# A bound by one broadcast minimum, and a subtraction moved into the bias of the exponentials, in the scan of a hybrid diffusion trunk

## The chip, the cores and the metric

The kernel runs on one core of a Trainium2 chip (trn2). The metric is the device time of one execution, in microseconds (us). Engines are named as in the profile: PE is TensorE, PEld its weight loads, DVE is VectorE, ACT is ScalarE, POOL is GpSimd, and SP issues the DMAs.

## The reference

Two layers over 512 latent and 256 context tokens with 1024 channels: layer 0 mixes tokens by a bidirectional Mamba-2 scan (SSD), layer 1 by neighbourhood attention, and each is followed by a squared-ReLU MLP. The part that matters here is one chunk of 128 tokens of the scan. Per direction there are 32 heads in 4 groups of 8; `dtc` is the step size after the softplus and `a` is negative, so `cum` falls along a chunk:

```python
cum = jnp.cumsum(dtc * a, axis=1)
seg = cum[:, :, None] - cum[:, None, :]
decay = jnp.exp(jnp.where(mask, seg, -jnp.inf))
cb = jnp.einsum('bign,bjgn->bijg', cc, bc)
scores = cb[..., None] * decay * dtc[:, None]
y = jnp.einsum('bijge,bjgep->bigep', scores, xc)
```

## The kernel before

Tokens lie in the free dimension and channels on partitions, in 6 chunks of 128 tokens. All large products are made of three float32r products of split operands: a unit of weights (1024 rows, 128 columns) comes by DMA as `raw`, ACT rounds it to `wh` (L112), and DVE subtracts to get `wl` (L113); PE then runs 48 matmuls on it (L137), 24 with 512 columns and 24 with 256. `wh` and `wl` have two buffers each, so the split for a unit waits until PE has left the unit two before it.

The SSD layer walks the units of the input projection, `w_in`. A unit ends in a convolution and Silu (`conv_unit`, L542 to L549) or in a Silu and a gate (`z_unit`, L681, then `gate`, L670 to L675). Between the matmuls of each unit, `unit` advances a generator, `scan`, by three steps. So the scan of one group of heads runs beside the projections of the next. A scan has 29 steps; the last 18 hold the work inside the chunks, three for each chunk.

Inside a chunk the weights are formed by `decays`, for four heads and both directions at once, so 12 times for each group and 48 times in all. The tile `E` is [128, 2, 4, 128]: partition j, direction, head, token i. Two DMAs (L609) fetch `cum` of the tokens i for four heads, from `crow` in DRAM, spread over all partitions. Eight DVE instructions (L613), one for each direction and head, subtract the column `colb` = cum_j - ln dt_j and take the minimum with the column `lnd` = ln dt_j; without that bound the masked half could overflow. One ACT instruction (L615) takes the exponential of all 1024 columns. Then `G`, the masked product of C and B, is multiplied in, for direction 0 by DVE (L616) and for direction 1 by POOL (L617), and POOL adds the two (L618). PE multiplies the sum by the inputs `xtok` (L639). `E` has three buffers, and a call of `decays` is made one ahead of its use.

Beside it a chunk has: the product of the carried states `sf` and `sb` with C (L651, fp32), its scaling by `eb` (L653, DVE), the sum `y` (L655 DVE, L657 POOL), the inputs weighted for the next state (`xw`, L582, POOL), their product (L584) and the state's step (L594, L595, DVE).

The order on each engine is fixed when the program is built, by a scheduler that works from the program's order and its own estimates; weight splits go ahead with high priority. The engine queues run in that order, so an instruction that waits holds all that stands behind it.

Of the kernel before, what the change touches and what calls it, by code (L numbers as in the profile page):

```python
# [7 lines left out]
F32 = mybir.dt.float32  # L8
# [5 lines left out]
P = 128  # L14
# [14 lines left out]
# column layout of the small-parameter array  # L29
# [7 lines left out]
# column layout of the constants  # L37
# [3 lines left out]
# order in which the column blocks of ssd_w_in (past dt) are walked  # L41
XBC_ORDER = []
for _g in range(GROUPS):
    XBC_ORDER += [16 + _g, 24 + _g, 20 + _g, 28 + _g]  # B fwd, B bwd, C fwd, C bwd
    XBC_ORDER += [4 * _g + _i for _i in range(4)]
# blocks whose residual sums go to GpSimd
# [5 lines left out]
def trunk(ctx: ExitStack, tc: tile.TileContext, a, out, dbg=None, stop=None):  # L52
# [14 lines left out]
    def psum(**tags):  # L67
        """Cuts PSUM anew: a pool per tag, of the given number of buffers."""
        if psums:
            psums["stack"].close()  # L70
        psums["stack"] = st = ctx.enter_context(ExitStack())
        for tag, bufs in tags.items():
            psums[tag] = st.enter_context(tc.tile_pool(name=f"ps_{tag}", bufs=bufs, space=bass.MemoryType.PSUM))
# [18 lines left out]
    # rows 0, 32 and 64 are ones: spreads row 32 j of a tile over all partitions  # L92
# [23 lines left out]
    class Units:  # L116
        """Walks the 128-column units of a weight array."""
# [24 lines left out]
    def ln_exp_tables(after):  # L142
        """Loads the table set with both Ln and Exp once the instruction `after` is issued."""
# [4 lines left out]
    # silu(c) and silu(c_ctx), side by side for each block of 128 channels  # L148
# [8 lines left out]
    def mod_unit(ps, q, raw):  # L157
        """Unit q of the weights of a chunk of 512 columns: half q // 2 of the columns, blocks 4 (q % 2) + j of the rows,
        whose products go to the partitions 32 j and 32 j + 1 (and others into those behind), so that the four run at once."""
# [6 lines left out]
    def mod_finish(l, ch, ps, cp, row_pool=None):  # L166
        """The four parts of the sums ps plus the bias, into columns."""
# [24 lines left out]
    def mod_pieces(chunks, pool_):  # L192
        """The same in four pieces a chunk, as a generator that yields after each."""
# [18 lines left out]
    def mod(l, i, s):  # L212
        """Column [128, 8] of modulation term i for stream s (0 latent, 1 context)."""
# [12 lines left out]
    def scaled(name, l, n, i, plus1):  # L226
        """g[n] * (m_i + 1) or g[n] * m_i, as [128, 8, 2]."""
# [6 lines left out]
    def rsqrt_into(r, t, ms):  # L234
        """r = ms^-1/2 where ms holds mean + eps already; t is scratch."""
# [6 lines left out]
    # Values per token are kept on [96, 256]: tokens 256 j .. on partitions 32 j .. 32 j + 31.  # L242
    xsq = const.tile([96, 256], F32, name="xsq")  # mean square of the residual stream
# [4 lines left out]
    def row_sums(ps, js, terms):  # L248
        """ps [96, 256], rows j = sums over the partitions and over the terms [128, 256] that terms(j) lists, for j in js."""
# [10 lines left out]
    def spread(js, src, into):  # L260
        """into[:, tokens j] = row j of src, on all partitions."""
# [5 lines left out]
    class Sums:  # L267
        """Sums over the blocks of a sub-layer's output y, per partition and token: y^2, x y' and y'^2, where
        y' = y times the column factors and x the residual stream. The last block's share stays apart."""
# [6 lines left out]
        def add(self, o, y, yp, x, G, s0, s1, final=False):  # L276
            """Block o: yp[:, o] = y * G, and the sums."""
# [13 lines left out]
        def factors(self, js, pre=None, final=False):  # L291
            """R and r for the token ranges js: x + y' R is the stream after the sub-layer, r the factor of its
            rmsnorm. Moves xsq on. pre: y still lacks the factor pre per token."""
# [9 lines left out]
            else:  # L303
                # rmsnorm(pre * v) = v * pre / sqrt(pre^2 mean(v^2) + eps)
# [23 lines left out]
    def add_block(k, y, x, R, sl):  # L328
        """x += y' R for block k and the tokens sl."""
# [4 lines left out]
    def modulate(k, b, x, r, A, sh, s, hh, hl):  # L334
        """hh + hl = x * r * A + sh for block k; b is scratch."""
# [4 lines left out]
    def join(y, x, sums, sl, A, s, hh, hl):  # L340
        """x += y' R, hh + hl = x A for the tokens sl. What the norm still wants, times r and plus the shift, comes behind
        the product with the weights."""
# [17 lines left out]
    def shift_cols(l, i, at, hh, hl):  # L360
        """The columns at and at + 1 of hh + hl: the shifts of both streams."""
# [14 lines left out]
    # ================= layer 0: mixer input =================  # L376
# [58 lines left out]
    # ================= layer 0: SSD =================  # L435
# [12 lines left out]
    # dt: softplus, decays  # L448
    colb = dk.tile([P, NCH, 64], F32, name="colb")
    lnd = dk.tile([P, NCH, 64], F32, name="lnd")  # L450
# [19 lines left out]
    # log1p(e) = 2 atanh(e / (2 + e))  # L470
# [17 lines left out]
    dve.scalar_tensor_tensor(dta, dtv, -1.0, arow.unsqueeze(1).broadcast_to([P, NCH, 64]), ALU.mult, ALU.mult)  # L488
    lndf = lnd.rearrange("p c q -> p (c q)")
    dve.tensor_scalar(lndf, dt, 1.0e-37, None, op0=ALU.max)  # L490
    act.activation(lndf, lndf, AF.Ln)
    # running sums inside each chunk: forward from its start, backward from its end
# [4 lines left out]
    cum = ssd.tile([P, NCH, 64], F32, tag="sf", name="cum", bufs=2)  # L497
# [9 lines left out]
    dve.tensor_tensor(colb, cum, lnd, ALU.subtract)  # L507
# [21 lines left out]
    def unit(acc, n):  # L529
        """One unit of w_in, with n steps of the scan on the way."""  # L530
# [6 lines left out]
    def conv_unit(xb, tag, bufs, n=3):  # L537
        """One 128-channel block of silu(conv(h @ w_in) + b)."""
# [746 lines left out]
```

## Time and profile before

| what | value |
|---|---|
| runs shown | 2261.58 us median of 3 (2261.01, 2261.58, 2269.79) |
| span of the profiled execution | 2267.4 us; its own time isn't listed apart from the three runs, whose range the span lies in |
| PE busy over the span | 94% |
| DVE, ACT, POOL busy | 59%, 41%, 24% |
| mean granted clock of PE | 0.967 |

The span counts from the first to the last instruction. Busy shares are averages over stages: the scan stage takes the time from about 100 to 700 us, then come the MLP of layer 0, the attention and the second MLP. The rows below name lines by their numbers in the kernel before; those of the changed kernel lie one or two lines further down.

### The profile page before, as it was taken

What the parts mean: (1) busy time and instruction counts of PE and PEld (TensorE: products, weight loads), DVE (VectorE), ACT (ScalarE), POOL (GpSimd) and SP (SyncE); (2) the same over time, 40 slices, a digit from 0 to 9 for tenths busy, and PEclk for the clock granted to TensorE, in tenths of its full rate; (3) what the DMA queues carried; (4) which work ended last, traced back from release to release, by engine and by line L of the source; (5) the groups of instructions that cost most, each with busy time, mean ns of one, the idle gap of its engine ahead of it and who ended that gap; (6) DMA issues with size and microseconds to landing.
All of it is one profiled execution on the core that took longest, in us unless ns stands there. A gap on an engine that the chain in (4) does not pass through costs nothing.

```text
span 2267.4 us, 32646 instructions
## 1 busy us (share of the span) xinstructions
PE 2135.5 (94%) x12848; PEld 1761.0 (78%) x12848; DVE 1337.9 (59%) x2311; ACT 931.3 (41%) x1405; POOL 552.5 (24%) x434
## 2 busy tenths in 40 slices
PE   6999999989979988999999999799999989999996
PEld 3787777867868766888888888578788768899896
DVE  5758878688584787314334244677666665344355
ACT  4544534544333653223123134355555543333244
POOL 0024645253462562000000003612212170000003
PEclk8999999999999998999999999799999899999998
DMA  7436757366565622333333111321110124222233
GB/s 262 137 131 187 211 167 215 112 176 189 182 184 188 213 75 75 112 112 113 116 114 110 61 65 58 112 69 35 54 52 33 38 75 140 93 93 92 95 103 112
DMA packets 136877, 269.73 MB, mean 119 GB/s; under 512 B 13074, under 2 KB 70804, under 8 KB 136724
## 3 DMA queue, kind: packets, MB, share of 16 engines
q1 hardware_dynamic: 136724, 267.65, 37.2%
q8 instruction: 101, 1.65, 0.3%
q14 instruction: 52, 0.43, 0.1%
HBM read 244.27 MB, written 23.33 MB: 118 GB/s over the span
## 4 chain that ended last, share of the span: by engine, by line
PE 77%; DVE 12%; POOL 3%; issue 3%; DMA 3%; ACT 2%; SPq 0%; DVEq 0%; ACTq 0%; POOLq 0%
PE acc L826 20%; PE acc L878 20%; PE acc L137 17%; PE a L965 5%; DVE E L613 4%; PE a L976 2%; DMA E<-crow 2%; PE sc L1023 2%; PE s L162 2%; PE pt L1037 1%; PE yp L1052 1%; PE sc L1022 1%; DVE wl L113 1%; PE s L584 1%; PE s L253 1%
## 5 line engine op out<-in xcount | busy, mean ns | idle before, releaser
L112 ACT ACTIVATE wh<-raw 128x1024 fp32r<-128x1024 f32 (+1 forms) x241 | 254.2, 1055 | 688.3 <-PE acc L878 311.2
L113 DVE TENSOR_TENSOR wl<-raw,wh 128x1024 fp32r<-128x1024 f32 (+1 forms) x241 | 316.7, 1314 | 242.7 <-ACT wh L112 239.6
L137 PE MATMUL acc<-hh,wh 128*128 128x512 f32 (+1 forms) x976 | 289.5, 373 | 0.0
L137 PE MATMUL acc<-hl,wh 128*128 128x512 f32 (+1 forms) x976 | 264.3, 346 | 0.0
L137 PE MATMUL acc<-hh,wl 128*128 128x512 f32 (+1 forms) x976 | 262.4, 344 | 0.0
L826 PE MATMUL acc<-hh,wh 128*128 128x258 f32 (+2 forms) x1024 | 243.2, 317 | 9.8 <-ACT hh L357 9.8
L878 PE MATMUL acc<-ah,wh 128*128 128x512 f32 (+1 forms) x832 | 248.2, 348 | 4.1 <-DVE ya L884 4.0
L878 PE MATMUL acc<-ah,wl 128*128 128x512 f32 (+1 forms) x832 | 245.3, 344 | 0.8 <-DVE wl L113 0.8
L878 PE MATMUL acc<-al,wh 128*128 128x512 f32 (+1 forms) x832 | 245.6, 345 | 0.0
L826 PE MATMUL acc<-hl,wh 128*128 128x258 f32 (+2 forms) x1024 | 241.8, 314 | 3.1 <-DVE hl L358 3.0
L826 PE MATMUL acc<-hh,wl 128*128 128x258 f32 (+2 forms) x1024 | 240.9, 313 | 0.0
L137 PEld LDWEIGHTS acc<-hh,wh 128*128 128x128 f32 (+1 forms) x976 | 156.6, 191 | 54.5 <-issue 36.5
L613 DVE TENSOR_SCALAR E<-E,colb,lnd 128x128 f32<-128x128 f32 x384 | 171.8, 506 | 35.1 <-DMA E<-crow 34.9
L826 PEld LDWEIGHTS acc<-hh,wh 128*128 128x128 f32 x1024 | 161.2, 192 | 33.9 <-issue 11.5
L289 POOL TENSOR_TENSOR syy<-syy,last 128x512 f32<-128x512 f32 (+2 forms) x24 | 38.1, 1588 | 582.2 <-ACT last L279 582.1
L826 PEld LDWEIGHTS acc<-hl,wh 128*128 128x128 f32 x1024 | 160.9, 191 | 17.4 <-DVE hl L358 5.0
L137 PEld LDWEIGHTS acc<-hh,wl 128*128 128x128 f32 (+1 forms) x976 | 153.9, 190 | 25.0 <-issue 1.4
L137 PEld LDWEIGHTS acc<-hl,wh 128*128 128x128 f32 (+1 forms) x976 | 154.5, 191 | 23.9 <-issue 0.8
L826 PEld LDWEIGHTS acc<-hh,wl 128*128 128x128 f32 x1024 | 161.9, 191 | 11.7 <-issue 0.7
L878 PEld LDWEIGHTS acc<-ah,wh 128*128 128x128 f32 x832 | 140.2, 190 | 32.8 <-issue 13.1
L884 DVE TENSOR_TENSOR ya<-ya,acc 128x768 f32<-128x768 f32 (+2 forms) x56 | 40.6, 725 | 198.0 <-PE acc L878 198.0
L878 PEld LDWEIGHTS acc<-ah,wl 128*128 128x128 f32 x832 | 140.2, 189 | 21.8 <-DVE wl L113 1.0
(317 smaller groups left out, 3837.2 us busy)
## 6 DMA issues: line engine op xcount, KB each, us to landing
raw<-in_w_dram SPq DMA_DIRECT2D x136, 512.0 KB, 3.4
mraw<-in_modw_dram SPq DMA_DIRECT2D x72, 512.0 KB, 3.3
raw<-in_win_dram SPq DMA_DIRECT2D x48, 512.0 KB, 3.9
E<-crow SPq DMA_DIRECT2D x96, 256.0 KB, 5.2
eb<-erow SPq DMA_DIRECT2D x96, 128.0 KB, 3.7
raw<-in_wout_dram SPq DMA_DIRECT2D x24, 512.0 KB, 3.4
raw<-in_modw_dram SPq DMA_DIRECT2D x8, 1024.0 KB, 17.6
raw<-in_wqk_dram SPq DMA_DIRECT2D x16, 512.0 KB, 3.3
```

The costliest lines, as they stand in the source:

```text
L112: act.activation(wh[:, :n], raw[:, :n], AF.Copy)
L113: dve.tensor_tensor(wl[:, :n], raw[:, :n], wh[:, :n].bitcast(F32), ALU.subtract)
L137: pe.matmul(acc[:m, s0:s1], lhsT=ww[:, i * m:(i + 1) * m], rhs=xx[:, k, s0:s1], start=first and i == 0 and j == 0, stop=last and i == len( ...
L162: mm = pe.matmul(ps[32 * j:32 * j + 32, hf * 256:hf * 256 + 256], lhsT=cact[:, 8 * kg + 2 * j:8 * kg + 2 * j + 32], rhs=raw[:, j * 256:j * ...
L289: pool.tensor_tensor(t[:, s0:s1], t[:, s0:s1], d, ALU.add)
L613: dve.tensor_scalar(E[:, d, e], E[:, d, e], colb[:, c, q:q + 1], lnd[:, c, q:q + 1], op0=ALU.subtract, op1=ALU.min)
L826: pe.matmul(acc[:, d0:d0 + s1 - s0], lhsT=ww[wi], rhs=xx[:, k, s0:s1], start=k == 0 and j == 0, stop=k == KB - 1 and j == 2)
L878: pe.matmul(acc[:, s0:s1], lhsT=ww[:, k * P:(k + 1) * P], rhs=xx[:, s0:s1], start=k == 0 and j == 0, stop=k == KB - 1 and j == 2)
L884: dve.tensor_tensor(y, y, acc[:, p0:p1], ALU.add)
L965: pe.matmul(acc[:, :s1 - s0], lhsT=ws[ww][:, k * P:(k + 1) * P], rhs=xx[:, k, s0:s1], start=k == 0 and j == 0, stop=k == KB - 1 and j == 2)
L976: pe.matmul(acc, lhsT=xx[:, k, i * P:(i + 1) * P], rhs=w[ww][:, sl], start=k == 0 and n == 0, stop=k == KB - 1 and n == 2)
L1023: pe.matmul(ps[:, o:o + 256], lhsT=Q[2][own, qs], rhs=K[par][own, ks], start=False, stop=True)
```

## The change

`decays` bounds the exponent before the subtraction instead of behind it: min(cum_i, cum_j) is taken for all 1024 columns in one DVE instruction, with `cum` of the partition's own token as an operand that is repeated along i (a stride of zero). The rest of the exponent, `ncol` = ln dt_j - cum_j, is a value per partition, direction and head, and goes into the exponential as its bias; one ACT instruction then covers only the 128 columns of one head and direction, so there are eight. The product with `G` is one DVE instruction over 1024 columns, and POOL keeps the sum alone. For the tiles, `cum` takes the place of `lnd` among those that are kept, and `ncol` that of `colb`.

```diff
-    colb = dk.tile([P, NCH, 64], F32, name="colb")
-    lnd = dk.tile([P, NCH, 64], F32, name="lnd")
+    ncol = dk.tile([P, NCH, 64], F32, name="ncol")
+    cum = dk.tile([P, NCH, 64], F32, name="cum")
...
+    lnd = ssd.tile([P, NCH, 64], F32, tag="sf", name="lnd", bufs=2)
...
-    cum = ssd.tile([P, NCH, 64], F32, tag="sf", name="cum", bufs=2)
...
-    dve.tensor_tensor(colb, cum, lnd, ALU.subtract)
+    dve.tensor_tensor(ncol, lnd, cum, ALU.subtract)
...
             E = ssd.tile([P, 2, 4, P], F32, tag="E", name="E", bufs=3)
             for d in range(2):
                 q0 = d * 32 + g * 8 + hf * 4
                 sp.dma_start(E[:, d], crow[c, q0:q0 + 4].partition_broadcast(P))
+            h0 = g * 8 + hf * 4
+            own = cum[:, c].rearrange("p (d q) -> p d q", d=2)[:, :, h0:h0 + 4].unsqueeze(3)
+            dve.tensor_tensor(E, E, own.broadcast_to([P, 2, 4, P]), ALU.min)
             for d in range(2):
                 for e in range(4):
-                    q = d * 32 + g * 8 + hf * 4 + e
-                    dve.tensor_scalar(E[:, d, e], E[:, d, e], colb[:, c, q:q + 1], lnd[:, c, q:q + 1],
-                                      op0=ALU.subtract, op1=ALU.min)
-            act.activation(E, E, AF.Exp)
-            dve.tensor_tensor(E[:, 0], E[:, 0], G[c][:, 0:1].broadcast_to([P, 4, P]), ALU.mult)
-            pool.tensor_tensor(E[:, 1], E[:, 1], G[c][:, 1:2].broadcast_to([P, 4, P]), ALU.mult)
+                    q = d * 32 + h0 + e
+                    act.activation(E[:, d, e], E[:, d, e], AF.Exp, bias=ncol[:, c, q:q + 1], scale=1.0)
+            dve.tensor_tensor(E, E, G[c].unsqueeze(2).broadcast_to([P, 2, 4, P]), ALU.mult)
             pool.tensor_tensor(E[:, 0], E[:, 0], E[:, 1], ALU.add)
```

The scheduler then sets other orders. In the scan of the second group, beside the second of its `z_unit` calls, DVE's queue (wl is the next weight split, zt the gate, y, eb and sf the chunk's output and state) stood before as:

```order
L113 TENSOR_TENSOR wl_3097<-raw_3094,wh_3096 128x1024
L613 TENSOR_SCALAR E_3042<-E_3042,colb_421,lnd_422 128x128 x4
L670 TENSOR_TENSOR zt_2940<-zt_2940,sq_2942 128x768
L655 TENSOR_TENSOR y_2999<-y_2999,s_2902 128x512
L613 TENSOR_SCALAR E_3042<-E_3042,colb_421,lnd_422 128x128 x3
L653 TENSOR_TENSOR eb_2897<-eb_2897,s_3001 128x512
L613 TENSOR_SCALAR E_3042<-E_3042,colb_421,lnd_422 128x128
L653 TENSOR_TENSOR eb_2897<-eb_2897,s_3007 128x512
L613 TENSOR_SCALAR E_3112<-E_3112,colb_421,lnd_422 128x128
L595 TENSOR_TENSOR sf_3021<-sf_3021,s_3019 128x512
L613 TENSOR_SCALAR E_3112<-E_3112,colb_421,lnd_422 128x128 x4
L616 TENSOR_TENSOR E_3042<-E_3042,G_2307 128x512
```

and now stands as:

```order
L113 TENSOR_TENSOR wl_3077<-raw_3074,wh_3076 128x1024
L613 TENSOR_TENSOR E_2956<-E_2956,cum_422 128x1024
L671 TENSOR_TENSOR zt_2922<-zt_2922,sq_2924 128x768
L656 TENSOR_TENSOR y_2980<-y_2980,s_2885 128x512
L654 TENSOR_TENSOR eb_2880<-eb_2880,s_2982 128x512
L613 TENSOR_TENSOR E_3023<-E_3023,cum_422 128x1024
L654 TENSOR_TENSOR eb_2880<-eb_2880,s_2988 128x512
L595 TENSOR_TENSOR sf_3002<-sf_3002,s_3000 128x512
L618 TENSOR_TENSOR E_2956<-E_2956,G_2295 128x1024
L613 TENSOR_TENSOR E_3092<-E_3092,cum_422 128x1024
L618 TENSOR_TENSOR E_3023<-E_3023,G_2295 128x1024
L113 TENSOR_TENSOR wl_3213<-raw_3210,wh_3212 128x1024
```

The pieces of the old minimum lay spread between the other instructions; the new ones are whole, and a third call's minimum has moved ahead of the next weight split. ACT's queue at the same place was:

```order
L112 ACTIVATE wh_3096<-raw_3094 128x1024
L681 ACT_TABLE_LOAD
L681 ACTIVATE zt_2940<-acc_2823 128x768
L674 ACTIVATE sq_2942<-zt_2940 128x768
L615 ACT_TABLE_LOAD
L615 ACTIVATE E_3042<-E_3042 128x1024
L615 ACTIVATE E_3112<-E_3112 128x1024
L112 ACTIVATE wh_3234<-raw_3232 128x1024
```

and is now:

```order
L112 ACTIVATE wh_3076<-raw_3074 128x1024
L682 ACT_TABLE_LOAD
L682 ACTIVATE zt_2922<-acc_2807 128x768
L617 ACT_TABLE_LOAD
L617 ACTIVATE E_2956<-E_2956,ncol_421 128x128
L675 ACTIVATE sq_2924<-zt_2922 128x768
L617 ACTIVATE E_2956<-E_2956,ncol_421 128x128 x7
L617 ACTIVATE E_3023<-E_3023,ncol_421 128x128 x8
L617 ACTIVATE E_3092<-E_3092,ncol_421 128x128 x6
L112 ACTIVATE wh_3212<-raw_3210 128x1024
```

Where two exponentials stood between two splits of weights, 22 stand now, of two whole calls and most of a third. Over the program ACT's queue holds 70 table loads, and held 58.

## Rows read from the trace of the kernel before

**Rows 1.** The page: busy time of each engine, its share of the span, instructions

```profile
PE 2135.5 (94%) x12848; PEld 1761.0 (78%) x12848; DVE 1337.9 (59%) x2311; ACT 931.3 (41%) x1405; POOL 552.5 (24%) x434
```

**Rows 2.** Busy time by engine in the four scan stretches together, all instructions

```profile
sum 311.40, PE 268.39 PEld 213.30 DVE 276.94 ACT 140.78 POOL 178.16; mean PE 67.10 PEld 53.33 DVE 69.23 ACT 35.19 POOL 44.54
```

**Rows 3.** The same stretches, instructions on tile E alone: length, busy (count), then PEclk, DMA

```profile
195.60:268.00 72.40, 6.35 (x72) 3.93 (x72) 35.60 (x79) 9.20 (x9) 29.85 (x18) 0.95 0.77 222
300.50:371.30 70.80, 5.87 (x72) 3.75 (x72) 39.14 (x72) 8.48 (x8) 23.30 (x15) 0.95 0.66 197
455.00:547.00 92.00, 8.16 (x88) 5.18 (x88) 49.70 (x90) 10.60 (x10) 30.35 (x18) 0.91 0.68 189
611.00:687.20 76.20, 7.20 (x82) 4.51 (x80) 38.14 (x72) 8.47 (x8) 26.75 (x16) 0.96 0.66 183
```

**Rows 4.** Chain of work inside the stretch 455 to 547 us, shares by line

```profile
by line: DVE E L613 26.9%; DMA E<-crow 14.6%; issue 10.4%; PE acc L137 6.1%; PE s L651 5.7%; POOL E L618 5.5%; DVE eb L653 4.8%; DMA eb<-erow 4.1%; PE s L639 3.9%; DVE wl L113 3.1%; DVE sf L595 2.6%; POOL ssqy L675 2.0%; DVE sf L594 2.0%; D
```

**Rows 5.** Waits of PE, 90 to 720 us: line, releaser, total, times, longest

```profile
PE s L639 <- POOL E L618: 33.0, 16, 5.3
```

**Rows 6.** Timeline of PE, 488 to 530 us: start, duration, line, [idle before, releaser]

```profile
508.12 1.12 PE L639 MATMUL s<-E,xtok 128*64 128x128 f32 x8 [5.32 <-POOL E L618]
...
517.72 0.52 PE L137 MATMUL acc<-hl,wh 128*128 128x512 f32 x2
...
522.30 0.51 PE L137 MATMUL acc<-hh,wl 128*128 128x512 f32 x2
...
524.06 0.66 PE L639 MATMUL s<-E,xtok 128*64 128x128 f32 x8 [1.25 <-POOL E L618]
...
524.65 0.63 PE L137 MATMUL acc<-hh,wh 128*128 128x512 f32 x2
...
525.81 1.05 PE L651 MATMUL s<-cTt,sf 128*128 128x128 f32 x8
...
528.81 0.51 PE L137 MATMUL acc<-hl,wh 128*128 128x512 f32 x2
```

**Rows 7.** Timeline of DVE, same stretch

```profile
516.69 4.71 DVE L613 TENSOR_SCALAR E<-E,colb,lnd 128x128 f32<-128x128 f32 x12
...
524.48 2.31 DVE L113 TENSOR_TENSOR wl<-raw,wh 128x1024 fp32r<-128x1024 f32 x1
```

**Rows 8.** Timeline of ACT, same stretch

```profile
494.83 0.85 ACT L674 ACTIVATE sq<-zt 128x768 f32<-128x768 f32 x1 [2.45 <-DVE zt L670]
...
507.18 1.28 ACT L681 ACT_TABLE_LOAD   x1
...
508.47 0.81 ACT L681 ACTIVATE zt<-acc 128x768 f32<-128x768 f32 x1
...
521.92 1.06 ACT L615 ACTIVATE E<-E 128x1024 f32<-128x1024 f32 x1 [2.53 <-DVE E L613]
...
522.89 1.04 ACT L112 ACTIVATE wh<-raw 128x1024 fp32r<-128x1024 f32 x1
```

**Rows 9.** Groups by line and shape, whole span: busy us, mean ns | idle before

```profile
L613 DVE TENSOR_SCALAR E<-E,colb,lnd 128x128 f32<-128x128 f32 x384 | 171.8, 506 | 35.1 <-DMA E<-crow 34.9
...
L616 DVE TENSOR_TENSOR E<-E,G 128x512 f32<-128x512 f32 x48 | 47.0, 984 | 13.9 <-ACT E L615 13.2
...
L113 DVE TENSOR_TENSOR wl<-raw,wh 128x1024 fp32r<-128x1024 f32 x240 | 316.1, 1317 | 242.7 <-ACT wh L112 239.6
...
L617 POOL TENSOR_TENSOR E<-E,G 128x512 f32<-128x512 f32 x48 | 81.4, 1701 | 215.8 <-DVE G L565 156.6 <-ACT E L615 59.2
...
L549 ACT ACTIVATE zt<-xT,dtot 128x768 f32<-128x768 f32 x16 | 15.0, 936 | 0.4
...
L546 ACT ACTIVATE xT<-xT 128x768 f32<-128x768 f32 x16 | 13.5, 846 | 13.4 <-DVE xT L545 13.1
...
L992 ACT ACTIVATE v<-a 128x128 fp32r<-128x128 f32 x36 | 9.8, 273 | 19.5 <-DVE v L993 15.9 <-PE a L976 3.4
```

**Rows 10.** The page, DMA issues: count, KB each, us to landing

```profile
E<-crow SPq DMA_DIRECT2D x96, 256.0 KB, 5.2
```

## The prediction, made before the changed kernel was run

> **What bounds the kernel now.** Read the page first: PE is busy for 94% of the span [rows 1], so an engine beside it matters only where PE waits for it. The scan stage has four such stretches, one for each group, in which the chunks' inner work runs: 195.6 to 268, 300.5 to 371.3, 455 to 547 and 611 to 687.2 us. There the picture turns over: of 311.4 us DVE is busy for 276.9 and PE for 268.4, while ACT and POOL have 140.8 and 178.2 [rows 2]. The reader is to see that DVE has 89% of these stretches and that 162.6 us of it is work on E alone, the sum of the third busy column of [rows 3]. The clock that PE was granted there is 0.95, 0.95, 0.91 and 0.96 [rows 3]. Next the chain of waits: in the third stretch its largest share is the DVE line that bounds the exponents, 26.9%, and then the DMA that fills E, 14.6% [rows 4]. From PE's side it is one wait, for POOL's sum that ends E's making: 33.0 us in 16 waits [rows 5], for instance 5.32 us before 508.12 [rows 6].
>
> The unit of time is one unit of weights, which carries two calls of `decays`. The two waits at 508.12 and 524.06 are one unit apart: 15.9 us. PE needs less. The 13 steps from 517.72 to 522.30 are two matmuls each, so 0.352 us a pair, and the 24 pairs of a unit take 8.45. The four heads of a call take 0.59 (524.06 to 524.65), twice 1.18. From 525.81 to 528.81 lie the products with both states, the product for the next state and one pair, so 3.00 - 0.35 = 2.65 [rows 6]. Together 12.3 us. The stretches hold 72 + 72 + 88 + 82 = 314 records of the heads' matmuls [rows 3], 16 to a unit: 19.6 units, and 311.4 / 19.6 is 15.9 again. So at most (15.9 - 12.3) x 19.6 = 71 us lie there; between them the chain of waits runs through PE's own products, and E's making is hidden behind those.
>
> **The change, part by part.** *DVE, removed.* The eight bounds and the half product cost 171.8 + 47.0 us of busy time for 48 calls [rows 9], 4.6 us a call or 9.1 a unit. *DVE, added.* Two instructions over 1024 columns with both inputs in SBUF. The weight split is such an instruction: 1.32 us in the mean [rows 9], and 2.31 while POOL is at work [rows 7]. Four of them cost 5.3 to 9.2 us a unit; I take 1.6 each, 6.4, nearer the mean since POOL has less to do. *POOL, removed.* 81.4 us over 48 calls, 1.70 each [rows 9], which lay between exponential and sum; the whole product on DVE, 1.6, takes its place there. The repeated operand and the swap of `cum`, `lnd`, `ncol` and `colb` cost nothing that isn't in these durations: the subtraction for the columns is made once, one for one.
>
> *ACT, added.* A call had one instruction of 1.06 us, 0.97 from start to start (521.92 to 522.89 [rows 8]). Eight of 128 columns take its place. Without a bias column such an instruction took 0.273; a scaling column made 768 columns cost 936 in place of 846 ns, 0.09 more [rows 9]. So 0.36 each, and 0.27 if they overlap by the 0.09 seen between 521.92 and 522.89. I take 0.32, between the ends, because the 0.273 is for a source in PSUM and this one is in SBUF; 16 a unit are 5.1 us, between 4.4 and 5.8. The order also has 12 more table loads of 1.28 us, 15 us of ACT in all, which fall where ACT has room unless a split waits behind them.
>
> *What stands in a new unit.* PE 12.3. DVE: a split, the gate, y, two eb, two state steps and the four E instructions. Without the E work DVE has (276.9 - 162.6) / 19.6 = 5.8 us a unit; with it 12.2, between 11.1 and 15.0. ACT: split 1.0, Silu 0.81, square 0.85, two loads 2.56, exponentials 5.1, together 10.3. No engine alone reaches 15.9, but they are coupled: 22 exponentials now stand between two splits, each call's wait for its minimum, and the square waits for DVE's gate as now, 2.45 us [rows 8]. One contended minimum of 1.8, between 1.32 and 2.31, is not covered by earlier exponentials, since its exponentials stand next in ACT's queue and the split of the weights behind them, and PE wants those weights a unit later. So a new unit is 10.3 + 2.45 + 1.8 = 14.6 us, and the gain is (15.9 - 14.6) x 19.6 = 25.5, about **26 us**. What is late next is the split of the weights, behind ACT's exponentials.
>
> *A wait added.* The minimum waits for both DMAs of E at once, where the first four bounds waited for one. Behind it on DVE stand the gate and the split. DVE waits for these DMAs for 34.9 us now [rows 9]; the second half starts a fraction of a microsecond behind the first, so I add nothing and keep it within the range.
>
> The sum is made against the profiled execution: 2267.4 - 26 = 2241 of span. That span is 5.8 above the median of the runs shown and inside their range. The saving is taken off the median: 2261.6 - 26 = 2235.6 us.
>
> *A rule weighed.* The trace has a table load start at 507.18 with no idle time before it and the Silu start at 508.47, 1.29 us later [rows 8]. The Trainium skill, "ScalarE: Activation LUTs", section "What ACT_TABLE_LOAD costs", gives 1283 ns for the load and about 1380 ns of drain, 2.66 us for each switch of sets. Here the trace agrees with the load and shows no drain. By the page a unit's two loads would cost 2.8 us more, 17.4 in place of 14.6, and the whole would be (17.4 - 15.9) x 19.6 = 29 us slower.
>
> **The rivals.** *PE alone sets the pace (0.14).* If ACT and DVE keep out of each other's way, a unit takes PE's 12.3 and the saving is 71 us: 2191 us. For it: ACT has 10.3 and DVE as little as 11.1. Against it: the order puts exponentials, products and splits in one line.
>
> *E's buffers set the pace (0.14).* A tile of E comes back every 1.5 units, 23.9 us now. The work in its way is then DMA 5.2 [rows 10], minimum 1.6, table load 1.28, eight exponentials 2.6, product 1.6, POOL's sum about as its half product now, 1.7 [rows 9], heads 0.6: 14.6 us. If the waits between them stay at 9.3 us or more, nothing is gained, and the DMA's share of the chain, 14.6% [rows 4], grows in place of the bounds': 2262 us, give or take 8. Against it: the longest of these waits is for DVE, which is relieved.
>
> *The change doesn't relieve DVE (0.06).* If all four new instructions cost the 2.31 of a split beside POOL, 9.2 us a unit stand against 9.1 removed, and the time stays within 8 us of 2262.
>
> *ACT becomes the bound, slower (0.14).* The place is the next split behind the exponentials. Price: exponentials without overlap 5.8 in place of 5.1, a third table load in a unit 1.28, and the minimum at 2.31: 14.6 + 0.7 + 1.3 + 0.5 = 17.1 us a unit, (17.1 - 15.9) x 19.6 = 24 us slower, 2285 us. It decides from the point at which ACT's work and waits in a unit pass 15.9. For it: ACT's queue has more loads and splits behind more instructions. Against it: ACT is busy for only 45% of the stretches now [rows 2].
>
> **How the numbers follow.** The forecast has 0.52, its own range 8 to 45 us of saving: 12.3 + 1.3 to 15.5 us a unit. The range must hold the time 8 times in 10: it leaves out the slower case (0.14) and the far half of the PE case (0.07), and reaches to 2202, 60 us of saving, and to 2268, the upper end of the two cases without a gain, with their 0.20. About 0.5% (11 us) is what a measurement of this kernel can tell from no change. Faster by more: 0.48 of the forecast, 0.14 of PE's case and 0.02 of the others, 0.64. Within it: 0.04 of the forecast and 0.18 of the two cases without a gain, 0.22. Slower: 0.14.
>
> **What would show it.** Right: in the four stretches DVE's busy time falls by 20 to 60 us and POOL's by some 60, ACT's rises by about 60; the exponentials come 0.32 us apart; the heads' waits for POOL shrink from 33 us; the units come about 14.6 us apart; the stretches' clock rises. Wrong, towards PE: units of 12 to 13 us and no wait of the heads left. Wrong, towards the buffers: DVE idle for E's DMA well over 35 us. Wrong, towards ACT: PE waits for `wl`, which it doesn't now, and DVE idles before the split for ACT's `wh` inside the stretches.

## The result: slower, and the profile after

The changed kernel took 2287.61 us (median of 4 runs, 2285.6 to 2290.32) beside 2262.08 for the kernel before: a ratio of 1.0109, 95% interval 1.009 to 1.0127. The forecast was 2235.6 us, 26 us faster; it came out 25.5 slower, above the range of 2202 to 2268. The profiled execution of the change has a span of 2288.5 us, 21.1 more than before, and a mean granted clock of 0.962 in place of 0.967.

The page, the row that answers to [rows 1]:

```profile
PE 2137.8 (93%) x12848; PEld 1761.1 (77%) x12848; DVE 1267.4 (55%) x1975; ACT 1014.1 (44%) x1753; POOL 504.0 (22%) x386
```

DVE fell by 70.5 us and POOL by 48.5, ACT rose by 82.8, as the change means them to. PE's own work is 2.3 us longer, so of the 21.1 us of span 18.8 are idle time of PE. The waits, 90 to 740 us (line, releaser, total, times, longest), say which:

```profile
DVE wl L113 <- ACT wh L112: 148.5, 37, 9.0
...
DVE E L613 <- DMA E<-crow: 64.8, 19, 7.2
...
PE s L640 <- POOL E L619: 53.2, 16, 9.8
```

PE's wait for the sum that ends E's making grew from 33.0 us [rows 5] to 53.2, by 20.2, which covers the 18.8. PE has no wait for `wl`. DVE now idles longer for E's DMA and for `wh` (34.9 and 103.1 us before): it was relieved by 70.5 us, and about as much became waiting.

Where this happens is seen in the stretches from the first call's heads (PE's products with `xtok`) to the end of the last call's, group by group. First before, the sum over its four stretches; then the change, stretch by stretch (busy time of PE, PEld, DVE, ACT, POOL, then PEclk, DMA share, GB/s):

```profile
sum 350.60, PE 305.90 PEld 242.68 DVE 300.68 ACT 155.06 POOL 189.75; mean PE 76.47 PEld 60.67 DVE 75.17 ACT 38.77 POOL 47.44
```

```profile
180.40:261.20 80.80, 73.66 (x481) 56.60 (x480) 58.08 (x68) 54.25 (x106) 32.70 (x20) 0.98 0.68 208
298.80:394.80 96.00, 81.67 (x498) 62.35 (x498) 60.77 (x63) 54.00 (x105) 40.69 (x23) 0.91 0.63 195
461.30:560.40 99.10, 74.90 (x442) 60.65 (x441) 62.05 (x56) 53.25 (x106) 43.54 (x24) 0.88 0.58 164
626.90:724.90 98.00, 82.66 (x478) 67.09 (x477) 60.42 (x56) 52.33 (x104) 38.78 (x22) 0.88 0.54 151
sum 373.90, PE 312.89 PEld 246.69 DVE 241.33 ACT 213.83 POOL 155.71; mean PE 78.22 PEld 61.67 DVE 60.33 ACT 53.46 POOL 38.93
```

These stretches are 23.3 us longer together, a little more than the whole span. In them DVE is busy for 65% of the time (241.3 of 373.9) and ACT for 57%: no engine beside PE is full, and still PE waits. The groups by line and shape, as [rows 9]:

```profile
L617 ACT ACTIVATE E<-E,ncol 128x128 f32<-128x128 f32 x384 | 120.5, 390 | 63.2 <-DVE E L613 32.1 <-issue 20.7 <-PE s L640 9.9
L619 POOL TENSOR_TENSOR E<-E 128x512 f32<-128x512 f32 x48 | 85.0, 1779 | 209.4 <-DMA raw<-in_win_dram 114.7 <-DVE E L618 54.8 <-ACT btok L566 26.3
L613 DVE TENSOR_TENSOR E<-E,cum 128x1024 f32<-128x1024 f32 x48 | 74.9, 1565 | 65.7 <-DMA E<-crow 64.8 <-POOL y L658 0.9
L618 DVE TENSOR_TENSOR E<-E,G 128x1024 f32<-128x1024 f32 x48 | 72.3, 1513 | 3.7 <-ACT E L617 3.7
L658 POOL TENSOR_TENSOR y<-y,eb 128x512 f32<-128x512 f32 x40 | 71.1, 1777 | 113.0 <-DVE eb L654 93.4 <-DMA yg_d<-zt 9.6 <-DMA E<-crow 8.9
...
L594 DVE TENSOR_TENSOR sf<-sf,dec 128x512 f32<-128x512 f32 x16 | 23.2, 1451 | 0.1
```

The two DVE instructions cost what was forecast, 1.57 and 1.51 us. The timelines show the turn. ACT (start, duration, line, [idle before, releaser]):

```profile
532.53 1.28 ACT L617 ACTIVATE E<-E,ncol 128x128 f32<-128x128 f32 x4 [4.98 <-issue]
533.72 1.04 ACT L112 ACTIVATE wh<-raw 128x1024 fp32r<-128x1024 f32 x1
534.78 1.28 ACT L682 ACT_TABLE_LOAD   x1
536.07 0.81 ACT L682 ACTIVATE zt<-acc 128x768 f32<-128x768 f32 x1
536.90 1.28 ACT L617 ACT_TABLE_LOAD   x1
538.20 0.40 ACT L617 ACTIVATE E<-E,ncol 128x128 f32<-128x128 f32 x1
538.51 0.83 ACT L675 ACTIVATE sq<-zt 128x768 f32<-128x768 f32 x1
539.24 0.98 ACT L617 ACTIVATE E<-E,ncol 128x128 f32<-128x128 f32 x3
545.60 2.44 ACT L617 ACTIVATE E<-E,ncol 128x128 f32<-128x128 f32 x8 [5.39 <-DVE E L613]
553.09 0.69 ACT L617 ACTIVATE E<-E,ncol 128x128 f32<-128x128 f32 x2 [5.05 <-PE s L640]
557.42 1.06 ACT L112 ACTIVATE wh<-raw 128x1024 fp32r<-128x1024 f32 x1 [3.63 <-PE acc L137]
...
559.26 1.85 ACT L617 ACTIVATE E<-E,ncol 128x128 f32<-128x128 f32 x6
```

Eight exponentials in a row take 2.44 us (545.60). But the call begun at 532.53 ends at 540.22, 7.69 us later: a weight split, a Silu, two table loads and a square stand among its eight. At 553.09 two are done, then the split of weights waits 3.63 us for PE to leave a buffer, with six exponentials behind it. DVE in the same stretch:

```profile
523.84 1.22 DVE L613 TENSOR_TENSOR E<-E,cum 128x1024 f32<-128x1024 f32 x1
524.98 1.22 DVE L618 TENSOR_TENSOR E<-E,G 128x1024 f32<-128x1024 f32 x1
...
530.13 2.31 DVE L613 TENSOR_TENSOR E<-E,cum 128x1024 f32<-128x1024 f32 x1
532.37 1.78 DVE L594 TENSOR_TENSOR sf<-sf,dec 128x512 f32<-128x512 f32 x1
...
544.34 1.22 DVE L613 TENSOR_TENSOR E<-E,cum 128x1024 f32<-128x1024 f32 x1 [6.46 <-DMA E<-crow]
...
546.68 1.92 DVE L618 TENSOR_TENSOR E<-E,G 128x1024 f32<-128x1024 f32 x1
```

The product at 546.68 belongs to the call whose exponentials ended at 540.22. It stands in DVE's queue behind a later call's minimum, which waits 6.46 us for its DMA. POOL's sum follows the product, and PE, which needs it, waits 9.76 us:

```profile
529.18 0.66 PE L640 MATMUL s<-E,xtok 128*64 128x128 f32 x8 [0.90 <-POOL E L619]
535.35 0.66 PE L640 MATMUL s<-E,xtok 128*64 128x128 f32 x8
551.98 1.12 PE L640 MATMUL s<-E,xtok 128*64 128x128 f32 x8 [9.76 <-POOL E L619]
```

So this wait comes from the order on DVE and from a late DMA, and not from the broken exponentials, which were done 6.5 us before the product began. The heads at 529.18 had freed the DMA's buffer at 529.84, but it stood in SP's queue behind the store of `y` and the DMAs for `eb`, and was issued 6.9 us later:

```profile
536.76 1.02 SPq L609 DMA_DIRECT2D E<-crow  x2
```

### The profile page after: what moved, and what is told of

The parts are those of the page before. It is cut to its first block, busy times and chain, and to the rows that moved or that the text cites. A ratio compares the mean times of both kernels' runs of the same rounds, so it can differ in the third digit from the quotient of the medians.

```text
span 2288.5 us, 32544 instructions
## 1 busy us (share of the span) xinstructions
PE 2137.8 (93%) x12848; PEld 1761.1 (77%) x12848; DVE 1267.4 (55%) x1975; ACT 1014.1 (44%) x1753; POOL 504.0 (22%) x386
## 4 chain that ended last, share of the span: by engine, by line
PE 69%; DVE 6%; POOL 3%; issue 2%; ACT 2%; DMA 1%; SPq 0%; DVEq 0%; POOLq 0%; ACTq 0%
PE acc L827 19%; PE acc L879 19%; PE acc L137 13%; PE a L966 5%; PE a L977 2%; PE sc L1024 2%; PE yp L1053 2%; PE pt L1038 1%; PE s L162 1%; PE sc L1023 1%; POOL sxy L289 1%; DVE ya L331 1%; DVE xa L332 1%; PE s L640 1%; POOL ssqy L289 1%
## 5 line engine op out<-in xcount | busy, mean ns | idle before, releaser
L113 DVE TENSOR_TENSOR wl<-raw,wh 128x1024 fp32r<-128x1024 f32 (+1 forms) x241 | 300.8, 1248 | 301.6 <-ACT wh L112 298.5
L137 PE MATMUL acc<-hl,wh 128*128 128x512 f32 (+1 forms) x976 | 269.4, 351 | 3.3 <-DVE hl L690 3.3
L879 PEld LDWEIGHTS acc<-al,wh 128*128 128x128 f32 x832 | 139.6, 189 | 20.1
```

What stands on the lines that cost most here:

```text
L113: dve.tensor_tensor(wl[:, :n], raw[:, :n], wh[:, :n].bitcast(F32), ALU.subtract)
L137: pe.matmul(acc[:m, s0:s1], lhsT=ww[:, i * m:(i + 1) * m], rhs=xx[:, k, s0:s1], start=first and i == 0 and j == 0, stop=last and i == len( ...
L879: pe.matmul(acc[:, s0:s1], lhsT=ww[:, k * P:(k + 1) * P], rhs=xx[:, s0:s1], start=k == 0 and j == 0, stop=k == KB - 1 and j == 2)
```

## The experiments

Three parts of the change can be set apart: M, the whole minimum in place of eight bounds; X, eight exponentials in place of one; G, the whole product on DVE. The times are medians of 4 to 10 executions, the ratios are to the kernel before, run beside each (2261.5 to 2263.5 us). e1, e5 and e6 leave out the subtraction of cum_j - ln dt_j, so they don't compute the output and show only what their instructions cost; e3's exponentials have no bias.

**One part at a time.** e1 is M and G:

```diff
-                    act.activation(E[:, d, e], E[:, d, e], AF.Exp, bias=ncol[:, c, q:q + 1], scale=1.0)
+            act.activation(E, E, AF.Exp)
```

> The changed kernel with one exponential over all 1024 columns and no bias, so the subtraction of cum_j - ln dt_j is left out of the computation; the broadcast minimum and the whole product on DVE stay. If the eight short exponentials on ACT are what costs (theory A), this is faster than the kernel before by 20 to 40 us, about 2225 to 2240. If it is the two whole DVE instructions, each of which holds the queue behind it until a DMA or ACT is done (theory B), it stays slower than before, 2270 to 2290.

Measured: 2266.59, ratio 1.002 [1.0011, 1.0029]. e2 is M and X; the product stays split between DVE and POOL:

```diff
-            dve.tensor_tensor(E, E, G[c].unsqueeze(2).broadcast_to([P, 2, 4, P]), ALU.mult)
+            dve.tensor_tensor(E[:, 0], E[:, 0], G[c][:, 0:1].broadcast_to([P, 4, P]), ALU.mult)
+            pool.tensor_tensor(E[:, 1], E[:, 1], G[c][:, 1:2].broadcast_to([P, 4, P]), ALU.mult)
```

> The changed kernel with the product shared between DVE and POOL as before; minimum and eight biased exponentials stay. Theory A: as slow as the changed kernel, 2280 to 2292. Theory B: some of the loss goes, 2262 to 2275. If the move of POOL's half product to DVE is the whole cause, 2240 to 2262.

Measured: 2274.82, 1.0054 [1.0036, 1.0071]. e3 is X alone, on the kernel before:

```diff
-            act.activation(E, E, AF.Exp)
+            for d in range(2):
+                for e in range(4):
+                    act.activation(E[:, d, e], E[:, d, e], AF.Exp)
```

> The kernel before with its exponential cut into eight of 128 columns without a bias, all else as before. Theory A: slower than before by 20 us or more, 2282 or more. Theory B: within 8 us of before, 2255 to 2270.

Measured: 2261.19, 0.9991 [0.9981, 1.0001]. Eight exponentials alone, without a bias, cost nothing. e4 is G alone, the diff of e2 the other way on the kernel before:

> The kernel before with the whole product on DVE and POOL keeping the sum alone. Theory A: DVE, which is the busiest engine in the stretches, gets 0.5 us more for a call and POOL 1.7 less, so within 10 us of before, 2252 to 2272. Theory B: slower by 5 to 20 us, since a product of 1024 columns holds what stands behind it.

Measured: 2248.52, 0.9931 [0.9914, 0.9947], faster. So with the eight bounds kept, G gains 14 us and X costs none. M on top of G takes the gain back (e1 is 18 above e4), and X on top of both costs another 21. G itself, a gain on the kernel before, costs 13 on top of M and X (the change beside e2). e1 and e4 lie outside the ranges of both theories, e2 and e3 in those of theory B.

**The form of the minimum.** e5 and e6 are e1 with the minimum in two halves, one for each direction, and in eight pieces of 128 columns; e9 is the whole change with the eight pieces:

```diff
-            dve.tensor_tensor(E, E, own.broadcast_to([P, 2, 4, P]), ALU.min)
+            for d in range(2):
+                for e in range(4):
+                    q = d * 32 + h0 + e
+                    dve.tensor_tensor(E[:, d, e], E[:, d, e], cum[:, c, q:q + 1].broadcast_to([P, P]), ALU.min)
```

> The minimum with the whole product on DVE and one exponential without a bias (subtraction left out, as in the first experiment, 2267), but the minimum in two instructions of 512 columns, one for each direction, each waiting for its own DMA. If the loss against the product alone (2249) comes from waiting for both DMAs and from one long instruction holding DVE (theory B), half of the 18 us or more come back, 2250 to 2258. If it comes from two-input instructions that run against POOL's sums (theory C), nothing changes, 2263 to 2271.

> The same with the minimum in eight instructions of 128 columns, cut as the kernel before cuts its bound; DVE's count and order become nearly those of the product alone (2249), only the form of the instruction differs (two tensors in place of a tensor and two columns). Theory B: 2246 to 2256. Theory C: 2260 to 2272.

> The changed kernel with its minimum in eight pieces of 128 columns; eight exponentials with bias and the whole product on DVE stay. Theory L (E's turn through its three buffers sets the pace, and a whole minimum lengthens the turn because it waits for both halves of E and holds other work behind it): the 20 us between the whole minimum and the one in pieces, seen with one exponential, come back here, 2268 us or less. Within it: if the eight exponentials cost something of their own once the whole product is on DVE, the time stays near 2267 (21 us over the version with one exponential, 2247); if they cost only where a whole minimum stands before them, 2247. Rival S (the eight exponentials and the weight split that falls between them make the change slow, whatever the minimum's form): 2280 to 2288.

Measured: e5 2253.51, 0.996 [0.9945, 0.9975]; e6 2246.69, 0.9932 [0.9918, 0.9947]; e9 2247.56, 0.9933 [0.9918, 0.9948]. The change with its minimum in pieces is 40 us faster than the change, and 15 faster than before; and X costs nothing again (e9 against e6). The page of e9, and its bound and product among the groups by line:

```profile
PE 2123.4 (94%) x12848; PEld 1750.1 (78%) x12848; DVE 1308.6 (58%) x2311; ACT 1015.7 (45%) x1753; POOL 480.9 (21%) x386
```

```profile
L615 DVE TENSOR_TENSOR E<-E,cum 128x128 f32<-128x128 f32 x384 | 131.0, 400 | 46.9 <-DMA E<-crow 46.8
...
L620 DVE TENSOR_TENSOR E<-E,G 128x1024 f32<-128x1024 f32 x48 | 69.9, 1464 | 6.8 <-ACT E L619 6.6
```

The pieces cost DVE 131.0 us where the whole minimum cost 74.9, and the kernel is 40 us faster: in these two kernels the busy time of DVE is not what this stage is short of. PE's wait for POOL's sum in e9, 90 to 740 us:

```profile
PE s L642 <- POOL E L621: 21.7, 12, 6.3
```

It is 31.5 us under the change's 53.2. Why pieces help, ACT's timeline of e9 shows:

```profile
493.88 1.28 ACT L619 ACTIVATE E<-E,ncol 128x128 f32<-128x128 f32 x4
495.95 0.40 ACT L619 ACTIVATE E<-E,ncol 128x128 f32<-128x128 f32 x1 [0.79 <-DVE E L615]
```

Exponentials start while DVE still makes later pieces of the same call; with a whole minimum all eight start behind its end. That this overlap is what the 40 us are is argued here, and f6 below speaks against it as the whole cause.

**Which wait.** e7 takes the store of `y` out of SP's queue, where it stood ahead of E's DMAs; f1 and f2 halve the minimum of the change, f1 by direction, so that a half needs one of E's two DMAs, f2 across, so that each needs both:

```diff
-            sp.dma_start(ypre[g * 4:(g + 1) * 4, :, cs].rearrange("j p i -> p j i"), y)
+            pool.dma_start(ypre[g * 4:(g + 1) * 4, :, cs].rearrange("j p i -> p j i"), y)
```

```diff
-            dve.tensor_tensor(E, E, own.broadcast_to([P, 2, 4, P]), ALU.min)
+            for k in range(2):
+                dve.tensor_tensor(E[:, :, 2 * k:2 * k + 2], E[:, :, 2 * k:2 * k + 2],
+                                  own[:, :, 2 * k:2 * k + 2].broadcast_to([P, 2, 2, P]), ALU.min)
```

> The changed kernel with the store of y issued from POOL, right behind the sum that it waits for, in place of SP, where E's DMAs stand behind it. If the loss runs through that wait (SP waits 113 us for POOL's sums in the changed kernel, 88 before; theory C's way to PE), the time falls by 15 us or more, to 2272 or less. If not, it stays within 8 us of 2288.

> The changed kernel with its minimum in two halves of 512 columns, one for each direction, so each half needs one of E's two DMAs and lets four exponentials go. Theory P (the whole minimum is slow because it stands as one block between DVE's wait and the first of the eight exponentials, while pieces let exponentials start under them): between the whole (2287.6) and eight pieces (2247.6), 2255 to 2270. Rival O (the whole minimum only happens to give a bad order, any other form a good one): 2250 or less.

> The changed kernel with its minimum in two halves of 512 columns, two heads of both directions in each, so that each half needs both of E's DMAs. It differs from the halves by direction in that alone. If the wait for both DMAs is what the whole minimum costs: 2275 to 2288, 10 or more above the halves by direction. Theory P: within 5 of the halves by direction, since the second DMA starts about a microsecond behind the first.

Measured: e7 2289.97, 1.0126 [1.0109, 1.0143], no change; f1 2263.38, 1.0 [0.9991, 1.001]; f2 2261.75, 0.9994 [0.9983, 1.0005]. Both halvings give 24 to 26 of the 40 us, so waiting for both DMAs is not the cost. e7 doesn't settle its question, for SP's wait stayed: in the change SP waits 113.4 us for POOL's `y` before the store, and in e7 101.8 us for the same sums before the DMAs into the one buffer of `eb`, which now stand ahead of E's. Against SP's queue as the cause of the loss speaks only that the mean time from a free buffer to its DMA's issue did not grow (2.1 us in the change, 2.8 before, in the table below).

**E's buffers.** Four buffers for E, and seven for `xtok` to make room: e8 on the change, e10 on e9, e11 on e4, e12 on the kernel before; f3 has the seven `xtok` alone.

```diff
-            E = ssd.tile([P, 2, 4, P], F32, tag="E", name="E", bufs=3)
+            E = ssd.tile([P, 2, 4, P], F32, tag="E", name="E", bufs=4)
...
-            xtok[c] = ssd.tile([P, 512], F32, tag="xtok", name="xtok", bufs=8)
+            xtok[c] = ssd.tile([P, 512], F32, tag="xtok", name="xtok", bufs=7)
```

> The changed kernel with four buffers of E in place of three (and seven of xtok in place of eight, for the room). If the way of a tile through its three buffers sets the pace (the rival of the prediction), the time falls by 15 us or more, to 2272 or less; if order or contention set it, within 8 us of 2288.

> The run with the minimum in eight pieces and eight exponentials, with four buffers for E (and seven for xtok, for the space). Theory L: with a buffer to spare the turn no longer sets the pace, so the minimum's form matters little: 2240 to 2255, as the changed kernel with four buffers (2255). Rival S: no faster than the changed kernel with four buffers by more than 3, and no faster than the run with three buffers beside it.

> The kernel before with the whole product on DVE and four buffers for E (seven for xtok). Theory L: the fourth buffer adds to what the product alone gave (2248.5): 2225 to 2240, and PE's waits for POOL's sum fall from 33 us to under 15. Rival D (DVE's busy time sets the pace): within 3 us of 2248.5.

> The kernel before with four buffers for E (seven for xtok), nothing else. Theory L: 2235 to 2252, with the heads' waits for POOL's sum well under 33 us. Rival D (DVE's busy time sets the pace, as the prediction had it): within 5 us of 2262, since DVE's work stays as it was.

> The kernel before with seven buffers for xtok in place of eight, and nothing else: the price of what made room for the fourth buffer of E. If E's turn through three buffers set the pace of the kernel before, the fourth buffer gained something that this price has hidden: 2270 to 2280. If the turn doesn't set it there: within 5 of 2262.

Measured: e8 2255.09, 0.9966 [0.9954, 0.9977]; e10 2256.35, 0.9972 [0.9961, 0.9982]; e11 2251.05, 0.996 [0.9944, 0.9975]; e12 2265.84, 1.0014 [1.0004, 1.0023]; f3 2262.31, 0.9995 [0.9985, 1.0004]. The fourth buffer takes 32 us off the change, and with it the form of the minimum no longer matters (e8, e10). On the kernels that were already faster it costs 2.5 and 9 us, on the kernel before it gains nothing, which I had not expected; f3 shows that the seven `xtok` don't hide a gain. The longest waits of PE, first before, then in e12, suggest why:

```profile
PE s L639 <- POOL E L618: 33.0, 16, 5.3
PE s L584 <- DVE y L655: 8.4, 3, 4.4
PE s L639 <- DVE y L655: 3.0, 2, 1.6
```

```profile
PE s L639 <- DVE y L655: 20.9, 6, 5.1
PE s L584 <- DVE y L655: 11.3, 5, 4.5
...
PE s L639 <- POOL E L618: 3.3, 2, 1.8
```

The 33.0 us for POOL's sum are down to 3.3, and those for DVE's `y` went from 11.4 to 32.2; all of PE's waits from 90 to 740 us are 45 us in both. So by these waits two limits lay side by side before the change, and taking one away gave nothing. e11 and e12 came out as the rival D of their expectations said, and not as theory L; but D, DVE's busy time as the pace, doesn't fit e9. e10 is 1 us above theory L's range and came out as rival S said of it, but S had e9 at 2280 or more.

**The order of the queues.** f4 is e9 with the product in two halves on DVE. f5 is the change with its exponentials at the scheduler's high priority, f6 is e9 with the same:

```diff
+            with tc.high_priority():
```

> The changed kernel with its minimum in eight pieces, and its product in two halves of 512 columns, one for each direction, both on DVE. Theory P, carried on: the first half of the product goes under the last four exponentials, so a turn gets shorter by up to the 0.9 us that now lie between exponentials and product: 2240 to 2248. If E's turn isn't what sets the pace once the minimum is in pieces: 2246 to 2256, with the second half's fixed cost on DVE.

> The changed kernel with the eight exponentials given the scheduler's high priority, as the weight splits have it; the minimum stays whole. In ACT's queue weight splits then stand inside 14 calls in place of 23, and other instructions inside a call are 14 in place of 106. Theory P (of the 40 us between the whole minimum and eight pieces about 20 come because the exponentials of a call, which a whole minimum lets go all at one point of the queue, are broken by other work, and 20 from the block on DVE): 2268 to 2277. If the block on DVE alone is the cause: 2283 to 2290. If the broken calls alone are: 2255 or less.

> The changed kernel with the minimum in eight pieces and the eight exponentials at high priority: splits stand inside 14 calls as against 13, other instructions inside a call are 52 in place of 67. Theory P: little to gain, 2243 to 2250, since the pieces let exponentials start under them already. If broken calls cost as much here as with a whole minimum: 2240 or less.

Measured: f4 2248.21, 0.993 [0.9914, 0.9945], nothing beyond e9; f5 2278.02, 1.0072 [1.0055, 1.0089], about 10 better than the change (its profiled execution took 2267.89 and is not read here); f6 2288.83, 1.0118 [1.0101, 1.0135]. f5 is 1 us above the range in which half of the 40 us come from broken calls. f6 is a miss of both theories: with nothing but a priority changed, the version in pieces lost its 40 us.

## Why the prediction was wrong

**The step that failed** is "So a new unit is 10.3 + 2.45 + 1.8 = 14.6 us". It added up what ACT does in a unit, with two waits, and took that for the pace. The stretches from first to last heads are 22 units long (four times 11 calls of half a unit): a unit takes 17.0 us, before 15.9. ACT is busy for 9.7 of it, near the 10.3, and idle for 7.3 (213.8 and 160.1 us over 22), where the sum had waits of 4.25. What paced the change in ACT's place is E's way through its three buffers, as far as e8 shows it; the prediction had that as a rival at 0.14 and put it aside with "the longest of these waits is for DVE, which is relieved". From the trace's records, for calls 4 to 12 of each group (36 calls), the mean time of each piece of a turn: from the heads that free the buffer to the DMA's issue ("free>"), to the minimum's start, and so on. ">exp" is from the end of the last bound to the first exponential; it and ">prod" are below zero where the steps overlap. Where the product is shared, "prod" is DVE's half, and POOL's lies in ">sum". The turns are of the profiled execution, the times medians.

```
        free>  issue>min  min  >exp   exp  >prod  prod  >sum   sum  >heads  heads   turn   median us
before   2.78     6.85   5.12  0.56  1.06   0.78  0.90  1.44  1.58   1.72   0.74   23.5   2262.1
change   2.11     7.34   1.54  0.80  5.19   1.71  1.56  1.25  1.75   1.88   0.78   25.9   2287.6
e1       3.18     7.92   1.49  0.49  1.06   1.26  1.65  0.77  1.90   2.87   0.72   23.3   2266.6
e2       2.17     7.86   1.67  0.93  3.40  -0.28  1.18  3.03  1.53   2.47   0.77   24.7   2274.8
e3       2.76     7.21   5.05 -3.40  4.28  -0.20  0.88  1.84  1.67   2.10   0.71   22.9   2261.2
e4       2.05     6.51   4.73  0.58  1.06   0.80  1.30  0.74  1.97   2.44   0.72   22.9   2248.5
e9       2.41     6.50   4.43 -2.49  4.34   0.87  1.44  0.43  1.61   2.06   0.72   22.3   2247.6
f1       1.95     6.25   3.05 -0.66  4.76   1.42  1.60  0.77  1.57   2.33   0.77   23.8   2263.4
f2       1.73     7.50   3.04 -1.27  5.47   1.48  1.41  0.67  1.60   1.84   0.76   24.2   2261.8
f6       3.10     6.70   4.10 -2.31  4.89   1.66  1.42  0.86  1.57   2.61   0.84   25.5   2288.8
```

The change made the turn 2.4 us longer. Its minimum is 3.58 us shorter from start to end, but the exponentials are 4.13 longer from first to last, and they no longer run under the bounds: from the minimum's start to the last exponential's end a turn takes 7.53 us, before 6.74, in e9 6.28. The wait for the product grew by 0.93, the product by 0.66, the time to the minimum by 0.49. Kernels with turns of 22.3 to 22.9 us lie at 2247 to 2261 (e5, e6 and f4, which aren't listed, too: 2246.7 to 2253.5), those of 23.3 to 24.7 at 2262 to 2275, those of 25.5 and 25.9 at 2288; inside these bands the order isn't kept. Counted so, from the heads of one call to those of the third after it, a turn is three times the pace whatever sets it, so the table shows where the time lies and not what sets it. For the change e8 tells more. Counted alike (calls 5 to 12), the way from the free buffer to the end of the sum takes 24.7 us with four buffers, 23.3 with three, so it got no shorter; but a call comes every 7.4 us (a turn of 29.6 through four) in place of 8.6, and the finished sum waits 4.25 us for its heads in place of 1.88. That is what one finds where the buffers set the pace. The scheduler made another order for e8 too, and what that alone does was not tried. That the turn isn't alone in the kernel before, e12 shows.

**Point by point.**
- *The two DVE instructions*, 1.6 us each: measured 1.57 and 1.51. Right.
- *The exponentials*, 0.32 us apart, 2.6 for eight: 2.44 where nothing comes between. But a weight split stands among a call's eight in 23 of 48 calls (e9 13, e3 8, counted in ACT's queue). Of the table's 36 calls 14 have one: they take 9.3 us from first to last, the other 22 take 2.6, and the mean is 5.19. This term of the rival's path was mis-sized: with 2.6 for them, and its waits unchanged, it gave 2262.
- *What is late next* was to be the split behind the exponentials. For PE it is the other way about: exponentials stand behind the split, which waits for PE, 3.63 us in the timeline and up to 8.5 in those 14 calls, 1.9 in the mean.
- *The wait added, "I add nothing"*: the wait for both DMAs costs nothing (f1, f2), although DVE's idle time before the bound rose from 34.9 to 64.8 us. In e1 DVE idles there for 79.5 us and the time is 2266.6: it marks a relieved engine, and not a loss by itself. But a late DMA costs where a product stands behind the minimum, as before the heads at 551.98; the wait for the product is in no term of the sum, and it grew by 0.93 us a turn.
- *The table loads*: no drain, as forecast; a load starts at 534.78 and the Silu behind it at 536.07, 1.29 us. With the drain that the prediction weighed, the kernel would have been 29 us slower; that this lies near the measured 25.5 is chance.
- *The slower rival* named 2285 us and had nearly the size, but its place is wrong, so the nearness is luck: PE waits for no `wl`, and ACT is busy for 57% of the stretches.
- *The signs named beforehand*: DVE's busy time fell by 59 us in the groups' stretches and ACT's rose by 59, as said; POOL's fell by 34 and not by 60. The waits for POOL and the clock went the wrong way, and DVE idle for E's DMA "well over 35 us" was the sign named for the buffers.

**What stays open.** The whole minimum costs 40 us against eight pieces in the order that the scheduler makes of each, and 24 to 26 of them go with two halves. How much of that is the block itself, which holds the queue behind it and lets no exponential start under it, and how much the order of three queues that comes with it, f6 leaves open: its turn is 3.1 us longer than e9's in small pieces, spread over its waits and its exponentials. What is shown is narrower: X and G alone do no harm, M takes back G's gain, X on top of a whole minimum costs 21 us and on top of pieces nothing, and a fourth buffer, with the order that comes with it, takes 32 us off the change. The fastest that compute all of the output, e9, f4 and e4, beat both kernels and lie within 1 us of each other; e9 keeps all of the change but the minimum's form, and gains no more than G by itself (e4).

## What to carry to other kernels

Before relieving a busy engine, add up one turn of each tile that goes round through few buffers, waits included, and look for slack in it: where a finished tile hardly waits for its user, the buffers may set the pace, and engine time saved off that path becomes idle time. A run with one more buffer is the test. One large instruction in place of eight saves busy time, but it gives up the overlap of its pieces with the next engine and holds all that stands behind it. Where a scheduler sets the queues, a gain of 1% can hang on the order alone, so the part and the order should each be tried by themselves.

## What the runs showed of the hardware

**A DVE instruction with two inputs in SBUF and one of POOL wait for each other.** In the DVE timeline above the same minimum takes 1.22 us at 523.84 and 2.31 at 530.13. POOL at these times:

```profile
524.99 2.92 POOL L676 TENSOR_TENSOR ssqy<-ssqy,sq 128x768 f32<-128x768 f32 x1 [10.47 <-ACT sq L675]
...
529.08 4.51 POOL L658 TENSOR_TENSOR y<-y,eb 128x512 f32<-128x512 f32 x2
...
539.41 1.83 POOL L676 TENSOR_TENSOR ssqy<-ssqy,sq 128x768 f32<-128x768 f32 x1 [4.11 <-ACT sq L675]
```

It was idle until the last 0.07 us of the first and adding at the second. POOL waits too: its add at 524.99 began 0.01 us behind the product of DVE at 524.98 and took 2.92 us, while the product took 1.22; the same add at 539.41, with DVE idle, took 1.83. A single piece of 128 columns in e9 shows the size of the wait best, DVE and then POOL:

```profile
492.77 1.85 DVE L615 TENSOR_TENSOR E<-E,cum 128x128 f32<-128x128 f32 x1
```

```profile
492.64 1.82 POOL L678 TENSOR_TENSOR ssqy<-ssqy,sq 128x768 f32<-128x768 f32 x1 [3.55 <-ACT sq L677]
```

It takes 1.85 us in place of 0.40 in the mean, and ends 0.16 after POOL's. The Trainium skill, "SBUF — State Buffer", section "Who interferes with whom", says that such a DVE instruction contends with a GpSimd one that reads SBUF; the trace agrees. The state's step `sf` (L594), which the change doesn't touch, takes 1451 ns in the mean, before 741 (768 in e9), and POOL's `y` 1777, before 1397; at 532.37 such an `sf` stands beside POOL's `y` and takes 1.78 us. That all of the rise comes from this is not shown.

**A wait costs PE twice.** Around the 9.76 us without work that end at 551.98, the windows of the change read (PEclk is third from the end):

```profile
535.00:542.00 7.00, 6.96 (x47) 5.52 (x45) 2.88 (x3) 5.17 (x8) 2.13 (x2) 1.00 0.81 160
542.00:548.00 6.00, 0.23 (x1) 0.00 (x0) 3.66 (x4) 2.40 (x8) 1.68 (x2) 0.85 0.81 294
548.00:552.00 4.00, 0.02 (x2) 0.02 (x2) 4.00 (x4) 0.04 (x1) 4.00 (x3) 0.50 0.25 70
552.00:556.00 4.00, 4.00 (x18) 3.28 (x19) 1.01 (x1) 0.69 (x2) 2.14 (x1) 0.50 0.84 193
556.00:562.00 6.00, 6.00 (x40) 5.00 (x40) 3.38 (x5) 3.69 (x8) 0.00 (x0) 0.97 0.36 118
```

The granted clock fell from 1.00 to 0.50, from 2.4 to 1.2 GHz, while PE stood still, and stayed there after work had come back: the heads at 551.98 took 1.12 us in place of 0.66. It works for a gain as well: of the 20.4 us by which e9's span (2247.0) is under that before (2267.4), 12.1 are PE's busy time, 2123.4 in place of 2135.5 for the same 12848 matmuls, at a mean clock of 0.973 in place of 0.967.
